# Two-layer decoder trunk: the high and low parts of an activation in one 512-column product

## The chip, the cores and the metric

The kernel runs on one core of one Trainium2 chip. Its time is the device time of one execution in microseconds (us); three executions of the kernel before took 362.71, 362.89 and 363.04 us, and 362.89 is the median that the changed kernel is held against. The profile is of one further execution; times in it count from its first instruction.

TensorE is called PE below (its loading of a stationary operand is PEld), VectorE DVE, ScalarE ACT, GpSimd POOL and the engine that issues the loads SP.

## The reference

256 tokens, model width 1024, two layers, all in float32. Each layer normalises the residual stream x, projects it, mixes tokens causally, multiplies by a SiLU gate z, projects back and adds; then a per-layer embedding p, projected to the model width, is gated by a sigmoid of the normalised stream and added:

```python
for i in range(DEPTH):
    h = rms_norm(x, norm_gain[i])
    x = x + (moba_layer(h, ...) if i % 2 == 0 else nsa_layer(h, ...))   # ends in: o @ w_out
    gate = jax.nn.sigmoid(rms_norm(x, ple_gate_gain[i]) @ ple_w_gate[i])
    x = x + gate * (p[i] @ ple_w_proj[i])
```

Layer 0 mixes with MoBA, which at 256 tokens is one causal block of 256 per head (16 heads of 64). Layer 1 mixes with NSA: a compressed branch, a selected-block branch and a window branch, gated per head; four groups of four heads share keys and values. Layer 1's softmax work is twice that of layer 0: two score matrices per head.

## The kernel before, in words

**Products in three parts.** A float32 weight W and a float32 activation X are each split into a high part, rounded to the fp32r type that PE multiplies in one pass, and a low part, the rest. The product is the sum of high W by high X, high W by low X and low W by high X. Weights are loaded 512 KB at a time into one of five `raw` tiles; ACT writes `hi` (five tiles), DVE subtracts and writes `lo` (five tiles); this is the "weight split". Activations are split likewise into `ah` and `al`, 128 features by 256 tokens each, nine tiles of either.

**Two kinds of products.** Those with tokens on the rows of the output (the projections to q, k and v) keep X still and stream 512 columns of W. Those with features on the rows (z, the projection of p, the output projection `o` and the gate `g`) keep a 128x128 block of W still and stream the 256 tokens of X, three products per block: lines 529 to 545, in class `Unit`. Such a unit makes 512 features out of eight k-blocks, in two PSUM banks `mm` of the four, each bank holding two 128-feature rows of results of 256 columns. The second gate unit of a layer (`apart=True`) holds its four rows in two `mm` banks and two score banks `s`.

**Evacuations.** `add_out` adds a bank of 512 columns of an `o` unit to x with one DVE instruction. `gate` multiplies a bank by the norm's factors `bc` (DVE), takes tanh (ACT), combines with the projected p and adds to x (DVE twice).

**What sets the order.** The program is written as a string of steps, `PROGRAM`, of which each records instructions. `w:o0.1` loads and splits the second weight block of layer 0's first output unit, `o0.1` multiplies with it, `o0>0` adds its first bank to x, `o0/1` is the rest of a unit for one bank; names of layer 1 begin with n. A planner (class `Plan`) then sets the order of each engine: it takes the step order as priority, gives each instruction a cost and a latency from its tables, and at each moment starts what can start first; copies marked as movable go to ACT or DVE as the planner chooses. Engines run their queues in order, so an early place in the DVE queue delays all that stands behind it. The steps are, for layer 0: the projections, `S` (scores and softmax), `T` (scaling and transposes), `V` (product with v), z, `x.k` (multiply by the gate and split), `o`, `b` (the norm), `y.k` (split for the gate), `g`; then `next.k` splits the stream for layer 1. Layer 1 runs `0S0` to `3S3`, `0T0` to `3T3`, the compression steps `KC`, `KD`, `W`, `WE`, and its own z, o and g.

In the transposes of layer 1, `sm` holds softmax weights, which DVE or ACT scale by `l1` (class `Group`, method `trans`) before PE transposes them. All the instructions carry line 396, a helper that emits them, so tiles' names tell them apart.

Of the kernel before, what the change touches and what calls it, by code (L numbers as in the profile page):

```python
# [8 lines left out]
F32R = mybir.dt.float32r  # L9
AF = mybir.ActivationFunctionType  # L10
OP = mybir.AluOpType
AX = mybir.AxisListType

P = 128
T = 256
D = 1024
KT = 8
# [2 lines left out]
SWITCH, POW = 150.0, 2300.0  # L20
NRAW, NHI, NLO, NPT, NA = 5, 5, 5, 9, 9
WARM = 16
MARGIN = 100.0

PROGRAM = ("x0 w:c0 x2 c0 x1 w:c1 c1 x3 w:c2 c2 x4 w:c3 w:c4 x5 c3 w:c5 w:k.0 x6 w:c6 consts x7 k.0 w:c7 c4 w:k.1 c5 "
# [22 lines left out]

STORES = 5

# [8 lines left out]
class View:  # L59


    def __init__(self, tile_, ap, steps=()):
        self.tile, self.ap, self.steps = tile_, ap, steps
# [354 lines left out]
def trunk(ctx: ExitStack, tc: tile.TileContext, a, out):  # L418
# [77 lines left out]
        return (hi.rearrange("p (a b) -> p a b", a=shape[0]), lo.rearrange("p (a b) -> p a b", a=shape[0]))  # L496

    def split_act(src, gain=None, either=False):
        hi = apool.tile([P, T], F32R, tag="ah", name="ah")
        lo = apool.tile([P, T], F32R, tag="al", name="al")  # L500
        if gain is None:
            nc.scalar.activation(hi, src, AF.Copy)
            nc.vector.tensor_tensor(lo, src, hi.bitcast(F32), op=OP.subtract)
        else:
            if either:
                nc.copy(hi, src, gain)
            else:
                nc.scalar.activation(hi, src, AF.Copy, scale=gain)
            nc.vector.scalar_tensor_tensor(lo, src, gain, hi.bitcast(F32), op0=OP.mult, op1=OP.subtract)
        return hi, lo  # L510

    class Unit:

# [15 lines left out]
            self.w[g] = split(self.src[g], (self.kg, self.n))  # L529

        def mul(self, w, j, k, b, ms=(0, 1), cols=None, parts=(0, 1, 2)):
            (wh, wl), (xh, xl) = w, self.xs[k]
            first, last = k == 0, k == self.nk - 1
            if self.feat:
                for m in ms:
# [6 lines left out]
            else:  # L542
                c0, c1 = cols or (0, self.n)
# [17 lines left out]
        def steps(self, name):  # L561

            for g in range(self.granules):
                todo[f"w:{name}.{g}"] = lambda g=g: self.weights(g)
                if g < self.whole:
                    todo[f"{name}.{g}"] = lambda g=g: self.step(g)
            for i in range(len(self.parts)):
                todo[f"{name}/{i}"] = lambda i=i: self.part(i)
            return self

    todo = {}
# [115 lines left out]
    def evac_z(zz, u, i, m, norm):  # L687
# [4 lines left out]
        nc.scalar.activation(th, zr, AF.Tanh, scale=0.5)  # L692
        nc.vector.scalar_tensor_tensor(flat(zz[:, m:m + 2]), flat(th), 1.0, flat(zr), op0=OP.add, op1=OP.mult)

    def tail(i, oT, pvs, zin, xz, norm, after):


# [27 lines left out]
        def add_out(u, b, m):  # L725
            nc.vector.tensor_tensor(flat(xT[:, m:m + 2]), flat(xT[:, m:m + 2]), u.ps[b], op=OP.add)

        def split_g(k):
            xg[k] = split_act(xT[:, k], pg[:, i, k:k + 1])

# [19 lines left out]
                    after(k)  # L750

        for h in range(2):
            u = Unit(zin[h], True, xz).steps(f"{n}z{h}")
            for b in range(2):
                todo[f"{n}z{h}>{b}"] = lambda u=u, b=b, m=4 * h + 2 * b: evac_z(zz, u, b, m, norm)
            u = Unit(a["ple_proj"][i, h], True, px, nk=2).steps(f"{n}p{h}")
            for b in range(2):
                todo[f"{n}p{h}>{b}"] = lambda u=u, b=b, m=4 * h + 2 * b: evac_p(u, b, m)
            u = Unit(a["w_out"][i, h], True, xo, close=2).steps(f"{n}o{h}")
            for b in range(2):  # L760
                todo[f"{n}o{h}>{b}"] = lambda u=u, b=b, m=4 * h + 2 * b: add_out(u, b, m)
            u = Unit(a["ple_gate"][i, h], True, xg, apart=h == 1, close=i if h else 2).steps(f"{n}g{h}")
            for j in range(len(u.parts)):
                todo[f"{n}g{h}>{j}"] = lambda u=u, j=j, m=4 * h + (j if h else 2 * j), w=2 - h: gate(u, j, m, w)
# [576 lines left out]
def _arrays(i):  # L1341
    import numpy as np

    def c(v):
        return np.ascontiguousarray(v)
# [31 lines left out]
    r["w1"] = c(i["nsa_cmp_w1"][0].reshape(2, 4, 4, P, 256).transpose(0, 1, 3, 2, 4).reshape(2, 4, P, 1024))  # L1377
    r["w2"] = c(i["nsa_cmp_w2"][0].reshape(2, 2, P, HD).transpose(2, 1, 0, 3))

    r["cst"] = _constants()  # L1380
    return r

# [58 lines left out]
```

## Time and profile before

| | |
|---|---|
| median of three runs | 362.89 us (362.71 to 363.04) |
| profiled execution, first to last instruction | 359.3 us; no other time of that execution is given |
| what the runs' median has beyond that span | 3.6 us |
| PE busy | 353.5 us, 98% |
| DVE busy | 323.9 us, 90% |
| ACT busy | 270.6 us, 75% |
| read from and written to HBM | 57.5 and 1.0 MB, 163 GB/s over the span |

A row of a group gives line, engine, operation, tiles written and read, shape, count, then the busy time, the mean duration in ns and the idle time of the engine before it with what ended that. Matmuls overlap in the records: a 256-column product is recorded with 283 ns or so, and the next starts long before its end, so that the distance from start to start is what one costs. A row of a timeline gives the start, the duration, the engine and the instruction, and behind it in brackets the idle time before. A row of stretches gives the busy time of each engine within a stretch of the span.

### The profile page before, as it was taken

What the parts mean: (1) busy time and instruction counts of PE and PEld (TensorE: products, weight loads), DVE (VectorE), ACT (ScalarE), POOL (GpSimd) and SP (SyncE); (2) the same over time, 40 slices, a digit from 0 to 9 for tenths busy, and PEclk for the clock granted to TensorE, in tenths of its full rate; (3) what the DMA queues carried; (4) which work ended last, traced back from release to release, by engine and by line L of the source; (5) the groups of instructions that cost most, each with busy time, mean ns of one, the idle gap of its engine ahead of it and who ended that gap; (6) DMA issues with size and microseconds to landing.
All of it is one profiled execution on the core that took longest, in us unless ns stands there. A gap on an engine that the chain in (4) does not pass through costs nothing.

```text
span 359.3 us, 7138 instructions
## 1 busy us (share of the span) xinstructions
PE 353.5 (98%) x2569; PEld 321.3 (89%) x2569; DVE 323.9 (90%) x799; ACT 270.6 (75%) x592; POOL 29.2 (8%) x26
## 2 busy tenths in 40 slices
PE   8999999999999999999999999999999999999995
PEld 6788888888999999999889998777998999999995
DVE  5999999999999975969999999989999999967965
ACT  5756699986999855937665699959978989956711
POOL 1034004300000000000003300003000000000010
PEclk9999999999999999999999999999999999999999
DMA  7987656433564353645643645177374333142112
GB/s 241 386 313 244 188 186 224 166 117 108 191 193 130 116 177 98 218 153 177 205 141 113 210 120 174 60 291 280 133 232 150 119 126 111 52 146 98 59 31 88
DMA packets 20771, 58.97 MB, mean 164 GB/s; under 512 B 2560, under 2 KB 6016, under 8 KB 20736
## 3 DMA queue, kind: packets, MB, share of 16 engines
q1 hardware_dynamic: 20160, 58.04, 48.9%
q10 hardware_dynamic: 576, 0.48, 0.4%
q8 instruction: 20, 0.33, 0.4%
q14 instruction: 15, 0.12, 0.1%
HBM read 57.46 MB, written 1.05 MB: 163 GB/s over the span
## 4 chain that ended last, share of the span: by engine, by line
PE 96%; DMA 2%; DVE 0%; SPq 0%; issue 0%; ACT 0%; DVEq 0%; ACTq 0%
PE mm L396 74%; PE tr L396 13%; PE s L396 10%; DMA tmp<-in_moba_in 1%; DMA gain_in<-in_gain_in 1%; DVE tmp L396 0%; SPq L396 0%; DVE hi L396 0%; ACT tmp L396 0%; DVEq L1436 0%; DVE xT L396 0%; ACTq L396 0%
## 5 line engine op out<-in xcount | busy, mean ns | idle before, releaser
L396 ACT ACTIVATE hi<-raw 128x1024 fp32r<-128x1024 f32 (+2 forms) x100 | 99.0, 1006 | 29.8 <-PE mm L396 22.3
L396 DVE TENSOR_TENSOR lo<-raw,hi 128x1024 fp32r<-128x1024 f32 (+2 forms) x100 | 115.1, 1159 | 5.5 <-ACT hi L396 4.5
L396 PE MATMUL mm<-al,hi 128*128 128x256 f32 x416 | 116.9, 287 | 0.0
L396 PE MATMUL mm<-ah,lo 128*128 128x256 f32 x416 | 114.5, 286 | 0.0
L396 PE MATMUL mm<-ah,hi 128*128 128x256 f32 x416 | 114.3, 286 | 0.0
L396 PEld LDWEIGHTS mm<-al,hi 128*128 128x128 f32 x416 | 79.3, 191 | 0.2
L396 PEld LDWEIGHTS mm<-ah,lo 128*128 128x128 f32 x416 | 78.0, 191 | 0.3
L396 PEld LDWEIGHTS mm<-ah,hi 128*128 128x128 f32 x416 | 77.8, 191 | 0.4 <-issue 0.2
L396 PE MATMUL mm<-hi,ah 128*128 128x512 f32 (+2 forms) x178 | 66.7, 379 | 0.5 <-ACT ah L396 0.4
L396 PE MATMUL mm<-hi,al 128*128 128x512 f32 (+2 forms) x178 | 66.1, 374 | 0.0
L396 PE MATMUL mm<-lo,ah 128*128 128x512 f32 (+2 forms) x178 | 63.8, 375 | 0.0
L396 ACT ACTIVATE sm<-sm,nb 128x128 f32<-128x128 f32 (+1 forms) x96 | 42.6, 446 | 6.6 <-DVE nb L396 6.2
L396 PEld LDWEIGHTS mm<-hi,ah 128*128 128x128 f32 x178 | 33.4, 188 | 6.4 <-DVE hi L396 0.7
L396 PEld LDWEIGHTS mm<-hi,al 128*128 128x128 f32 x178 | 33.4, 188 | 5.4 <-DVE al L396 0.2
L396 PEld LDWEIGHTS mm<-lo,ah 128*128 128x128 f32 x178 | 33.1, 188 | 5.4 <-DVE lo L396 0.3
L396 DVE CUSTOM_DVE_ANT_0 sm<-s,cst,nr_q 128x128 f32<-128x128 f32 (+1 forms) x96 | 36.2, 410 | 1.6 <-PE s L396 1.3
L396 ACT ACTIVATE pt<-tr 128x384 f32<-128x384 f32 x48 | 21.6, 482 | 3.9 <-PE tr L396 3.6
L396 PE MATMUL tr<-cst,sm 128*128 128x128 f32 x144 | 23.9, 274 | 0.0
L396 POOL TENSOR_TENSOR r_q<-r,neg_half 128x16 f32<-128x16 f32 x5 | 15.8, 3150 | 76.9 <-DVE r L396 76.9
L396 ACT ACTIVATE tmp<-tmp 128x512 f32<-128x512 f32 (+3 forms) x22 | 11.2, 517 | 13.6 <-DVE tmp L396 13.5
L396 PEld LDWEIGHTS tr<-cst,sm 128*128 128x128 f32 x144 | 17.1, 140 | 2.0 <-issue 0.4
L396 ACT ACTIVATE ah<-xT,gain_in 128x256 fp32r<-128x256 f32 x31 | 14.8, 499 | 4.8 <-DVE xT L396 3.7
(176 smaller groups left out, 535.0 us busy)
## 6 DMA issues: line engine op xcount, KB each, us to landing
raw<-in_moba_in SPq DMA_DIRECT2D x28, 512.0 KB, 4.4
raw<-in_nsa_in SPq DMA_DIRECT2D x24, 512.0 KB, 3.7
raw<-in_w_out SPq DMA_DIRECT2D x16, 512.0 KB, 3.5
raw<-in_ple_gate SPq DMA_DIRECT2D x16, 512.0 KB, 3.9
raw<-in_w SPq DMA_DIRECT2D x8, 512.0 KB, 4.1
raw<-in_ple_proj SPq DMA_DIRECT2D x4, 512.0 KB, 4.1
raw<-in_nsa_vs SPq DMA_DIRECT2D x4, 304.0 KB, 2.8
xT<-in_x SPq DMA_DIRECT2D x8, 128.0 KB, 3.8
```

Of the source, the lines that this page charges most:

```text
L396: getattr(getattr(self.nc, o.engine), o.method)(*[real(x) for x in o.args], **{k: real(x) for k, x in o.kwargs.items()})
```

## The change

The output projections `o0`, `o1`, `no0`, `no1` and the gates `g0`, `g1`, `ng0`, `ng1` are made by a new class `Wide`. High and low part of an activation now lie side by side in one tile `a` of 512 columns, and the high block of W is multiplied with both at once: one 512-column product into one whole PSUM bank (high-by-high in the first half, high-by-low in the second) and one 256-column product of the low block into the first half. A unit makes 256 features in two banks and takes two weight blocks; there are 16 of them, named `o0a`, `o0b` and so on. The last, `ng1b`, is left narrow: it streams high and low part one after the other into the same half. The two halves of a bank have to be added: `add_wide` adds each half to x with an instruction of its own; `gate_wide` copies the second half to SBUF (ACT), adds the first (DVE), and goes on as before, 256 columns at a time instead of 512 or 256. Weights of these units come from arrays laid out for them, 512 KB a load as before. z and the projection of p stay as they were.

The step order is new from the 61st step on; below stand two of its lines.

```diff
+WIDE, NARROW = "o0 o1 g0 g1 no0 no1 ng0 ng1", "ng1b"
...
-           "no1.1 no1/0 no1>0 ny.4 w:ng0.1 nb.1 w:ng1.1 w:ng1.2 nb.3 no1/1 no1>1 ny.7 nb.5 ng0.0 ny.3 ng0.1 nb.6 "
+           "nb.6 nb.7 ng0a.00 nb w:ng0b.0 ny.7 ny.5 w:ng0a.1 ng0b.00 w:ng1a.0 ng0a.01 ny.4 ng0b.01 ny.6 w:ng0b.1 ng0b.10 "
...
     def split_act(src, gain=None, either=False):
-        hi = apool.tile([P, T], F32R, tag="ah", name="ah")
-        lo = apool.tile([P, T], F32R, tag="al", name="al")
+        both = apool.tile([P, 2, T], F32R, tag="a", name="a")
+        hi, lo = both[:, 0], both[:, 1]
...
-        return hi, lo
+        return hi, lo, both.rearrange("p a b -> p (a b)")
...
+    class Wide:
+        def __init__(self, src, xs, wide=True):
+            self.src, self.xs, self.w, self.ps, self.wide = src, xs, {}, None, wide
+
+        def weights(self, g):
+            if self.ps is None:
+                self.ps = [bank("mm", 4) for _ in range(2)]
+            self.w[g] = split(self.src[g], (4, T))
+
+        def mul(self, g, m):
+            (wh, wl), s, o = self.w[g], slice(m * P, m * P + P), self.ps[m]
+            for j in range(4):
+                k = 4 * g + j
+                xh, xl, both = self.xs[k]
+                if self.wide:
+                    nc.tensor.matmul(o, wh[:, j, s], both, start=k == 0, stop=False, skip_group_check=True)
+                else:
+                    nc.tensor.matmul(o[:, :T], wh[:, j, s], xh, start=k == 0, stop=False, skip_group_check=True)
+                    nc.tensor.matmul(o[:, :T], wh[:, j, s], xl, start=False, stop=False, skip_group_check=True)
+                nc.tensor.matmul(o[:, :T], wl[:, j, s], xh, start=False, stop=k == KT - 1, skip_group_check=True)
...
+        def add_wide(u, b, m):
+            for c in (slice(0, T), slice(T, 2 * T)):
+                nc.vector.tensor_tensor(xT[:, m], xT[:, m], u.ps[b][:, c], op=OP.add)
+
+        def gate_wide(u, b, m):
+            ps, x, last = u.ps[b], xT[:, m], i == 1 and m == KT - 1
+            gr, th = tmp("gr")[:, :T], tmp("th")[:, :T]
+            for c, d in (((slice(0, P), slice(T, T + P)), (slice(P, T), slice(T + P, 2 * T))) if last
+                         else ((slice(0, T), slice(T, 2 * T)),)):
+                if u.wide:
+                    nc.scalar.activation(gr[:, c], ps[:, d], AF.Copy)
+                    nc.vector.tensor_tensor(gr[:, c], gr[:, c], ps[:, c], op=OP.add)
+                nc.vector.tensor_tensor(gr[:, c], gr[:, c] if u.wide else ps[:, c], n1.bc[:, c], op=OP.mult)
+                nc.scalar.activation(th[:, c], gr[:, c], AF.Tanh, scale=0.5)
+                nc.vector.scalar_tensor_tensor(th[:, c], th[:, c], 1.0, pp[:, m, c], op0=OP.add, op1=OP.mult)
+                nc.vector.tensor_tensor(x[:, c], x[:, c], th[:, c], op=OP.add)
+                if last:
+                    (nc.scalar if c.start else nc.sync).dma_start(out[:, m, c], xT[:, m, c])
...
```

Three places show what this makes of the engines' queues. Before, PE's queue in the first output unit of layer 0 holds triples: high and low part of an activation (`ah`, `al`) with a high weight block (`hi`), and the high part with the low block (`lo`), into one bank `mm`.

```order
L396 MATMUL mm_79<-ah_106,hi_127 128x256
L396 MATMUL mm_79<-al_115,hi_127 128x256
L396 MATMUL mm_79<-ah_106,lo_132 128x256
L396 MATMUL mm_81<-ah_106,hi_127 128x256
L396 MATMUL mm_81<-al_115,hi_127 128x256
L396 MATMUL mm_81<-ah_106,lo_132 128x256
```

Now, in the first output unit of layer 0, it holds pairs, with transposes of softmax weights (`tr<-cst,sm`) between the groups as before.

```order
L399 MATMUL tr_76<-cst_65,sm_70 128x128 x3
L399 MATMUL mm_80<-a_106,hi_118 128x512
L399 MATMUL mm_80<-a_106,lo_123 128x256
L399 MATMUL mm_80<-a_108,hi_118 128x512
L399 MATMUL mm_80<-a_108,lo_123 128x256
L399 MATMUL mm_80<-a_107,hi_118 128x512
L399 MATMUL mm_80<-a_107,lo_123 128x256
```

Two products of 256 columns became one of 512 in each pair; over the program 480 became 240, and nothing else of PE's queue changed in number.

The second place is the end of layer 1's attention on DVE: the last softmax work of the last group (`ISA sm`: a score block shifted and reduced), the last scalings by `l`, and weight splits (`lo<-raw,hi`). Before:

```order
L396 TENSOR_TENSOR lo_132<-raw_134,hi_127 128x1024
L396 ISA sm_68,nb_3_184<-s_165,cst_65,nr_q_156 128x128
L396 ISA nb_3_184 128x1
L396 ISA sm_68,nb_3_184<-s_166,cst_65,nr_q_156 128x256
L396 ISA nb_3_184 128x1
L396 TENSOR_TENSOR al_114<-big_90,ah_105 128x256
L396 TENSOR_TENSOR lo_130<-raw_137,hi_125 128x1024
L396 RECIPROCAL l_3_188<-l_3_188 128x4
L396 TENSOR_TENSOR al_115<-big_90,ah_113 128x256
L396 TENSOR_TENSOR l_3_188<-l_3_188,gt_104 128x4
L396 TENSOR_SCALAR sm_70<-sm_70,l_3_188 128x128
```

Now:

```order
L399 TENSOR_SCALAR sm_69<-sm_69,l_2_178 128x256
L399 TENSOR_TENSOR l_3_179<-l_3_179,gt_104 128x4
L399 TENSOR_SCALAR sm_72<-sm_72,l_3_179 128x128
L399 TENSOR_SCALAR sm_72<-sm_72,l_3_179 128x256
L399 TENSOR_SCALAR sm_71<-sm_71,l_3_179 128x128
L399 TENSOR_SCALAR sm_71<-sm_71,l_3_179 128x256
L399 TENSOR_TENSOR tmp_86<-mm_78,bc_135 128x512
L399 TENSOR_TENSOR lo_121<-raw_124,hi_117 128x1024
```

The weight splits between the last scores moved behind them. Counted over the DVE queue, of the 105 weight splits 75 stand before the first softmax instruction of layer 1 in both orders; 21 stood between that and the last scaling, now 17; 9 stood behind, now 13.

The third place is the gates of layer 1 on DVE behind the norm's factors, `bc`. Before, a gate is a product with `bc`, a combination with the projected p (`big`) and an addition to x, and no weight split stands behind `bc`:

```order
L396 COPY bc_144<-tr_75 128x256
L396 TENSOR_TENSOR tmp_86<-mm_78,bc_144 128x256
L396 TENSOR_TENSOR tmp_82<-mm_81,bc_144 128x256
L396 SCALAR_TENSOR_TENSOR tmp_85<-tmp_85,big_88 128x256
L396 SCALAR_TENSOR_TENSOR tmp_84<-tmp_84,big_88 128x256
L396 TENSOR_TENSOR xT_63<-xT_63,tmp_85 128x256
L396 TENSOR_TENSOR xT_63<-xT_63,tmp_84 128x256
L396 TENSOR_TENSOR tmp_83<-mm_79,bc_144 128x512
```

Now:

```order
L399 COPY bc_135<-tr_75 128x256
L399 TENSOR_TENSOR tmp_86<-tmp_86,mm_81 128x256
L399 TENSOR_TENSOR tmp_86<-tmp_86,bc_135 128x256
L399 SCALAR_TENSOR_TENSOR tmp_84<-tmp_84,big_88 128x256
L399 TENSOR_TENSOR tmp_82<-tmp_82,mm_80 128x256
L399 TENSOR_TENSOR xT_63<-xT_63,tmp_84 128x256
L399 TENSOR_TENSOR tmp_82<-tmp_82,bc_135 128x256
L399 TENSOR_TENSOR lo_119<-raw_126,hi_114 128x1024
```

Each gate has one more DVE instruction, and one weight split, for the last unit `ng1b`, stands between them. Behind `bc` DVE's queue holds 27 instructions of 256 columns, 6 of 128 and this split; it held 9 of 256 columns, 6 of 512 and 6 of 128.

More of the change, by code (lines that the diff above doesn't have):

```diff
@@ L22 @@
 WARM = 16
+WIDE, NARROW = "o0 o1 g0 g1 no0 no1 ng0 ng1", "ng1b"
 MARGIN = 100.0
-PROGRAM = ("x0 w:c0 x2 c0 x1 w:c1 c1 x3 w:c2 c2 x4 w:c3 w:c4 x5 c3 w:c5 w:k.0 x6 w:c6 consts x7 k.0 w:c7 c4 w:k.1 c5 "
[22 rows of a table removed]
+PROGRAM = ("x0 w:c0 x2 c0 x1 w:c1 c1 x3 w:c2 c2 x4 w:c3 w:c4 x5 c3 w:c5 w:k.0 x6 w:c6 consts x7 k.0 w:c7 c4 w:k.1 c5 a.1 a.3 "
[24 rows of a table added]
 STORES = 5
@@ L531, in mul @@
         def mul(self, w, j, k, b, ms=(0, 1), cols=None, parts=(0, 1, 2)):
-            (wh, wl), (xh, xl) = w, self.xs[k]
+            (wh, wl), (xh, xl, _) = w, self.xs[k]
             first, last = k == 0, k == self.nk - 1
@@ L568, in steps @@
                 todo[f"{name}/{i}"] = lambda i=i: self.part(i)
+            return self
+    class Wide:
[16 more added lines that the diff above has]
+                nc.tensor.matmul(o[:, :T], wl[:, j, s], xh, start=False, stop=k == KT - 1, skip_group_check=True)
+        def steps(self, name):
+            for g in range(2):
+                todo[f"w:{name}.{g}"] = lambda g=g: self.weights(g)
+                for m in range(2):
+                    todo[f"{name}.{g}{m}"] = lambda g=g, m=m: self.mul(g, m)
             return self
@@ L693, in evac_z, with evac_wz @@
         nc.vector.scalar_tensor_tensor(flat(zz[:, m:m + 2]), flat(th), 1.0, flat(zr), op0=OP.add, op1=OP.mult)
+    def evac_wz(zz, ps, m, norm):
+        zr, th = tmp("zr")[:, :T], tmp("th")[:, :T]
+        nc.scalar.activation(zr, ps[:, T:], AF.Copy)
+        nc.vector.tensor_tensor(zr, zr, ps[:, :T], op=OP.add)
+        nc.vector.tensor_tensor(zr, zr, norm.bc, op=OP.mult)
+        nc.scalar.activation(th, zr, AF.Tanh, scale=0.5)
+        nc.vector.scalar_tensor_tensor(zz[:, m], th, 1.0, zr, op0=OP.add, op1=OP.mult)
     def tail(i, oT, pvs, zin, xz, norm, after):
@@ L726, in add_out, with wide @@
             nc.vector.tensor_tensor(flat(xT[:, m:m + 2]), flat(xT[:, m:m + 2]), u.ps[b], op=OP.add)
+        def add_wide(u, b, m):
[15 more added lines that the diff above has]
+                    (nc.scalar if c.start else nc.sync).dma_start(out[:, m, c], xT[:, m, c])
+            if not last:
+                after(m)
+        def wide(kind, h, xs, evac):
+            name = f"{n}{kind}{h}"
+            if name not in WIDE.split():
+                return False
+            for q in range(2):
+                u = Wide(a["w_" + name][q], xs, name + "ab"[q] not in NARROW.split()).steps(name + "ab"[q])
+                for b in range(2):
+                    todo[f"{name}{'ab'[q]}>{b}"] = lambda u=u, b=b, m=4 * h + 2 * q + b: evac(u, b, m)
+            return True
         def split_g(k):
@@ L752, in tail @@
         for h in range(2):
-            u = Unit(zin[h], True, xz).steps(f"{n}z{h}")
-            for b in range(2):
-                todo[f"{n}z{h}>{b}"] = lambda u=u, b=b, m=4 * h + 2 * b: evac_z(zz, u, b, m, norm)
+            if not wide("z", h, xz, lambda u, b, m: evac_wz(zz, u.ps[b], m, norm)):
+                u = Unit(zin[h], True, xz).steps(f"{n}z{h}")
+                for b in range(2):
+                    todo[f"{n}z{h}>{b}"] = lambda u=u, b=b, m=4 * h + 2 * b: evac_z(zz, u, b, m, norm)
             u = Unit(a["ple_proj"][i, h], True, px, nk=2).steps(f"{n}p{h}")
@@ L758, in tail @@
                 todo[f"{n}p{h}>{b}"] = lambda u=u, b=b, m=4 * h + 2 * b: evac_p(u, b, m)
-            u = Unit(a["w_out"][i, h], True, xo, close=2).steps(f"{n}o{h}")
-            for b in range(2):
-                todo[f"{n}o{h}>{b}"] = lambda u=u, b=b, m=4 * h + 2 * b: add_out(u, b, m)
+            if not wide("o", h, xo, add_wide):
+                u = Unit(a["w_out"][i, h], True, xo, close=2).steps(f"{n}o{h}")
+                for b in range(2):
+                    todo[f"{n}o{h}>{b}"] = lambda u=u, b=b, m=4 * h + 2 * b: add_out(u, b, m)
+            if wide("g", h, xg, gate_wide):
+                continue
             u = Unit(a["ple_gate"][i, h], True, xg, apart=h == 1, close=i if h else 2).steps(f"{n}g{h}")
@@ L1378, in _arrays @@
     r["w2"] = c(i["nsa_cmp_w2"][0].reshape(2, 2, P, HD).transpose(2, 1, 0, 3))
+    w = {}
+    for l, (n, z, lo) in enumerate((("", i["moba_w_in"][0], 3072), ("n", i["nsa_w_in"][0], 2608))):
+        w[n + "z"], w[n + "o"] = z[:, lo:lo + D], (i["moba_w_out"], i["nsa_w_out"])[l][0]
+        w[n + "g"] = i["ple_w_gate"][l]
+    for name in WIDE.split():
+        v = w[name[:-1]][:, 512 * int(name[-1]):][:, :512]
+        r["w_" + name] = c(v.reshape(2, 4, P, 2, T).transpose(3, 0, 2, 1, 4).reshape(2, 2, P, 4 * T))
     r["cst"] = _constants()
```

44 rows, old and new, of the table PROGRAM are left out of this document.

## The prediction

> **What bounds the kernel now.** I read the page's busy shares and its chain of waits first.
>
> ```profile
> span 359.3 us, 7138 instructions
> PE 353.5 (98%) x2569; PEld 321.3 (89%) x2569; DVE 323.9 (90%) x799; ACT 270.6 (75%) x592; POOL 29.2 (8%) x26
> DVE  5999999999999975969999999989999999967965
> PE mm L396 74%; PE tr L396 13%; PE s L396 10%; DMA tmp<-in_moba_in 1%; DMA gain_in<-in_gain_in 1%; DVE tmp L396 0%; SPq L396 0%; DVE hi L396 0%; ACT tmp L396 0%; DVEq L1436 0%; DVE xT L396 0%; ACTq L396 0%
> ```
>
> The chain lies on PE for nearly all of the span, so a shorter PE queue shortens the kernel as long as PE is fed. But DVE is at 90%, and its digits show where it has room: slices 15 to 18 and 35 to 40, which are the output and gate stages of the two layers. Elsewhere it stands at nine tenths or more. So I cut the span where layer 1's attention starts and ends on DVE, at its first softmax instruction (214.4) and its last scaling (315.1), with the view of stretches (total, then busy time of PE, PEld, DVE, ACT, POOL; then the granted clock).
>
> ```profile
> 0.00:214.40 214.40, 212.86 (x1431) 192.62 (x1432) 196.06 (x412) 160.20 (x303) 23.58 (x20) 1.00 0.57 185
> 214.40:315.10 100.70, 100.61 (x799) 89.80 (x799) 97.45 (x331) 90.84 (x255) 4.00 (x5) 1.00 0.46 156
> 315.10:359.30 44.20, 39.99 (x343) 38.90 (x341) 30.44 (x59) 19.55 (x35) 1.61 (x1) 0.99 0.26 83
> ```
>
> The middle stretch is level between two engines: PE has no idle time and DVE only 3.25 of 100.7 us. What DVE waited for there is in the view of waits for that window:
>
> ```profile
> DVE sm L396 <- PE s L396: 1.3, 2, 1.0
> DVE l L396 <- ACT sm L396: 0.5, 1, 0.5
> DVE hl L396 <- ACT qk_0r L396: 0.3, 1, 0.3
> ```
>
> 1.3 us of the idle time is DVE waiting for PE; the other 1.95 are ACT and gaps of about 30 ns between its own instructions, and would be there with an infinitely fast PE. So DVE alone needs 97.45 + 1.95 = 99.4 us of the 100.7. In this stretch a shorter PE queue gains next to nothing. In the last one DVE has 30.44 of 44.2: there PE sets the end.
>
> **The change: PE.** A product's price is the distance from start to start.
>
> ```profile
> 353.97 0.28 PE L396 MATMUL s<-al,hi 128*128 128x256 f32 x1
> 354.09 0.28 PE L396 MATMUL s<-ah,lo 128*128 128x256 f32 x1
> 354.21 0.28 PE L396 MATMUL s<-ah,hi 128*128 128x256 f32 x1
> 227.57 0.39 PE L396 MATMUL mm<-hi,ah 128*128 128x512 f32 x1
> 227.80 0.39 PE L396 MATMUL mm<-hi,al 128*128 128x512 f32 x1
> 228.03 0.39 PE L396 MATMUL mm<-lo,ah 128*128 128x512 f32 x1
> 228.25 0.39 PE L396 MATMUL mm<-hi,ah 128*128 128x512 f32 x1
> ```
>
> 256 columns cost 0.120 us and 512 cost (228.25 - 227.57) / 3 = 0.227. Both carry a fixed 0.013: 256 columns are half of 512, and 2 x 0.120 - 0.227 = 0.013. Merging two into one saves that, 240 times: 16 units of 8 k-blocks and 2 rows are 256, less 16 in the narrow unit. **Gain: 240 x 0.013 = 3.1 us.** Weight loads (one less per pair) cost nothing in either: they run under the product before, since the distances above already hold one each.
>
> TensorE: Matmul & The Clock Gate in the Trainium skill, section "Wait — 56ns, not 53.3ns?", puts the fixed cost of a matmul at about 2.5 ns once the clock is full. By that the merging would save 0.6 us and not 3.1, an estimate from that page. The rows above disagree, at a granted clock of 1.00, and the rows decide.
>
> The new order also mixes PE's queue otherwise. Transposes of softmax weights stand between products in runs; counted from the order there are 89 runs of such float32 work before and 77 now. A run of 6 and one of 3:
>
> ```profile
> 226.00 0.39 PE L396 MATMUL mm<-lo,ah 128*128 128x512 f32 x1
> 226.23 0.82 PE L396 MATMUL tr<-cst,sm 128*128 128x128 f32 x6
> 226.80 0.48 PE L396 MATMUL mm<-hi,ah 128*128 128x512 f32 x1
> 318.01 0.29 PE L396 MATMUL mm<-ah,hi 128*128 128x256 f32 x1
> 318.13 0.49 PE L396 MATMUL tr<-cst,sm 128*128 128x128 f32 x3
> 318.38 0.36 PE L396 MATMUL mm<-al,hi 128*128 128x256 f32 x1
> ```
>
> Six in one run take 0.80 - 0.227 = 0.57; three take 0.37 - 0.12 = 0.25, so twice three 0.50. One run fewer costs 0.07, twelve 0.9. Where a run has to wait for its softmax weights the advantage of a further run is gone, so the bounds are 0 and 0.9, and I take **+0.6**, as most runs in the trace stand like these.
>
> **The change: DVE.** The groups of DVE and the one of ACT that stand for the new work:
>
> ```profile
> L396 DVE TENSOR_TENSOR lo<-raw,hi 128x1024 fp32r<-128x1024 f32 x88 | 106.5, 1219 | 5.3 <-ACT hi L396 4.5 <-PE mm L396 0.4
> L396 DVE TENSOR_TENSOR xT<-xT,mm 128x512 f32<-128x512 f32 x8 | 5.5, 684 | 5.1 <-PE mm L396 5.1
> L396 DVE TENSOR_TENSOR tmp<-mm,bc 128x256 f32<-128x256 f32 x4 | 1.6, 419 | 0.0
> L396 DVE SCALAR_TENSOR_TENSOR big<-tmp,tmp 128x512 f32<-128x512 f32 x8 | 5.5, 683 | 0.0
> L396 DVE TENSOR_SCALAR sm<-sm,l 128x128 f32<-128x128 f32 x34 | 9.1, 279 | 0.1
> L396 DVE TENSOR_TENSOR al<-big,ah 128x256 fp32r<-128x256 f32 x16 | 6.2, 415 | 0.3
> L396 ACT ACTIVATE tmp<-tmp 128x256 f32<-128x256 f32 x7 | 2.8, 408 | 6.0 <-DVE tmp L396 6.0
> ```
>
> Output units: 32 additions of 256 columns from PSUM in place of 8 of 512: 32 x 0.42 - 8 x 0.68 = +8.0 us. The nearest row for such an addition is the product with `bc`, which also reads one PSUM operand of 256 columns. Gates: 14 further additions, 5.9, and the three older instructions of each gate in pieces of 256 in place of some of 512, 3 x 0.6. In all **+15.7 us of DVE** (11.3 if each overlaps its neighbour's end by 0.1, as queued pairs do), 339 us of a span of some 358. ACT gets 14 copies, 14 x 0.4 = +5.6, at 75%. Half of the new work falls into each layer's output and gate stage.
>
> Does it fit? Layer 0: it lies in the first stretch, where DVE has 18.3 us idle; some 4.6 go to the start, and 8 are added. I cost it at nothing; the cover is about 5 us, and beyond that each us of DVE would be one of PE. Layer 1: the last stretch had 13.8 idle. There the new order puts 4 weight splits (9 to 13) and these 8 us, so DVE's 30.4 become about 42.5, and the stretch itself grows, since PE's work moves there too. PE counts by the order: the middle stretch loses 104 products of 256 columns and gains 9 of 512, 104 x 0.120 - 9 x 0.227 = 10.4 us, while in front of 214.4 nothing changes in sum (the merging there pays for work drawn forward). So the last stretch grows by 10.4 - (3.1 - 0.6) = 7.9 to some 52 us, and DVE with 42.5 still fits.
>
> The middle stretch is the dear one. DVE there loses 4 weight splits (4.9), 2 SiLU combinations (1.4), 1 product of z with its norm (0.7), 2 gated outputs and their 2 splits (1.7), and gains 3 scalings (0.8), 3 copies of the compressed branch, and one subtraction (1.5): 6.4 less by these rows, 5.8 where they overlap; I take 6.0. DVE then needs 99.4 - 6.0 = 93.4 us with all its gaps, 91.5 without. PE's own work there was at most 100.6 and is 10.4 less, 90.2; with its waits for runs taken out, my count by distances is 99.0 before and 88.6 now. Before, PE lost 100.7 - 99.0 = 1.7 us in this stretch; now between 91.5 - 88.6 = 2.9 and 93.4 - 88.6 = 4.8. So the added wait of PE is **+1.2 to +3.1**. I take +1.6, near the lower end: the last scalings now follow each other with no weight split between, so PE runs products under them.
>
> DMA moves nothing in sum: 142 issues on SP in both, with the same sizes, and the landings of 4 us lie behind five buffers. The wait that is added is PE's for DVE; queued behind it on PE are the products of z and o, which are those that fill the time, and behind DVE's scalings the weight splits that PE needs next.
>
> **Sum:** -3.1 + 0.6 + 1.6 = **-0.9 us**, 359.3 to 358.4 in the span. The runs' median lies 3.6 above the profiled span, so 362.0. By the bounds: -3.1 + 0 + 0 gives 359.8, and -3.1 + 0.9 + 3.1 gives 363.8.
>
> **The rivals.** *PE's whole saving arrives.* If the planner's tight queue hides DVE in the middle stretch (ACT's waits there belonged to single places and may go), the term of 1.6 is 0 to 0.3: -2.5, 360.4. For it: DVE's idle time of before holds no long wait. Against it: 88.6 of PE against 91.5 of DVE.
>
> *Nothing is left.* The stretch takes its upper bound, 93.4: -3.1 + 0.6 + 3.1 = +0.6, 363.5. For it: the small gaps were all there before.
>
> *Slower: DVE's gates at the end.* Behind the norm's factors DVE had little to do:
>
> ```profile
> 345.11 0.38 PE L396 MATMUL tr<-cst,rstd 128*128 128x128 f32 x2
> 345.52 0.42 DVE L396 COPY bc<-tr 128x256 f32<-128x256 f32 x1 [2.22 <-PE tr L396]
> 349.74 0.69 DVE L396 SCALAR_TENSOR_TENSOR tmp<-tmp,big 128x512 f32<-128x512 f32 x1 [0.76 <-ACT tmp L396]
> 352.46 0.69 DVE L396 SCALAR_TENSOR_TENSOR tmp<-tmp,big 128x512 f32<-128x512 f32 x1 [0.70 <-ACT tmp L396]
> 354.81 0.28 PE L396 MATMUL s<-ah,lo 128*128 128x256 f32 x1
> ```
>
> Now 27 instructions of 256 columns (10.0 to 11.3 us) and a weight split (1.2) come between `bc`, 0.8 behind the transposes, and the last half-rows of 128 columns: 12.0 to 13.3 us. PE has behind the same transposes 25 pairs, 2 single products and 48 narrow ones: 25 x 0.347 + 50 x 0.120 = 14.7. That leaves 1.4 to 2.7. If each of eight gates waits for its tanh or its copy on ACT as the two rows show, 0.5 on average, 4 us are needed and DVE ends 2 late: 362.0 + 2.2 = 364.2. It decides from some 0.3 us of wait per gate. Against it: the new queue interleaves two or three gates, so one's wait is another's work.
>
> *Merging saves little.* The rows for 0.120 and 0.227 show products among their own kind; here 512 and 256 columns alternate. If a product of 256 that follows one of 512 starts some 0.0105 later than these rows let it, 240 x 0.0105 = 2.5 us of the 3.1 are lost, and the sum is -0.6 + 0.6 + 1.6 = +1.6, 364.5. No row of before shows such a late start. The same time would follow from the 2.5 ns of the Trainium skill (TensorE: Matmul & The Clock Gate, section "Wait — 56ns, not 53.3ns?"); the trace so far speaks against it.
>
> **How the numbers follow.** Forecast 0.44 (its own range 361.2 to 362.8), whole saving 0.16, nothing left 0.16, gates at the end 0.17, merging saves little 0.03, something else and slower 0.04. A measurement here tells about 0.2%, 0.7 us, from no change, so faster is below 362.2 and slower above 363.6. Faster: 0.16 and two thirds of the forecast, 0.46. Slower: 0.17 + 0.03 + 0.04 and a fifth of "nothing left", 0.27. Same: 0.27. The range runs from the lower bound, 359.7, to 364.4, which takes in most of the slower case.
>
> **What would show it.** In the changed profile: PE with 240 products of 512 columns at 0.227 and 256 behind them at 0.120 (else the first term is wrong); between layer 1's first softmax and last scaling 93 us in place of 100.7 with DVE idle under 2 (else the third); DVE busy 335 to 340 in all; the tail from PE's last product to the end still near 4.5 (else the gates). If DVE waits for PE in the middle stretch, PE still sets it and the gain is larger; if PE's queue shows stalls in layer 0's gates, the cover of 5 us was not there.

## The result: 1.9 us faster, and the profile after

Beside the kernel before, the changed kernel took 359.74 us against 362.89: a ratio of 0.9933 (0.9907 to 0.9958). Two later comparisons gave 0.9950 (0.9932 to 0.9967; 359.95 against 361.60) and 0.9955 (0.9938 to 0.9973; 360.09 against 361.62). (Each ratio is an estimate over the executions of both kernels and need not equal the quotient of the two medians, which is 0.9913 in the first comparison.) Weighted by their intervals the three make 0.9949, 1.9 us with some 0.4 either way. Two executions of all that were made, one of the run `noscale` with 433 us at a granted clock of 0.75 and one of the kernel before with 1981 us, are left out of every ratio. The forecast was 0.9 us less, at 362.0, within 359.7 to 364.4.

The first profile of the changed kernel, from the page: span, busy times, DVE in 40 slices, the chain of waits by line.

```profile
span 359.6 us, 6744 instructions
PE 353.2 (98%) x2329; PEld 308.7 (86%) x2329; DVE 335.5 (93%) x849; ACT 275.3 (77%) x610; POOL 27.7 (8%) x26
DVE  5799999999999988989999999999999999989975
PE mm L399 71%; PE tr L399 12%; PE s L399 6%; DMA xT<-in_x 2%; DVE lo L399 2%; DMA gain_in<-in_gain_in 1%; DVE q L399 1%; SPq L399 0%; DVE tmp L399 0%; DVE k_1r L399 0%; DVE hl L399 0%; DVE ssq L399 0%; DVE k_0r L399 0%; DVE kd_0r L399 0%; DVE v_1r L399 0%
```

DVE has 11.6 us more (11.3 were counted with overlaps), its roomy slices of the output and gate stages are filled, and PE still stands at 98%. The span is no shorter than the 359.3 of before, though. The reason lies in the executions that were profiled. For each execution of the changed kernel span and time are both known, and the time is always 1.74 to 1.82 above the span: this one took 361.40, the longest of its five; the others took 359.12 to 360.61. The kernel before, profiled a second time, has a span of 359.9 at a time of 361.65, 1.75 apart as well. So 359.3 belongs to some 361.1 us: the execution shown ahead of the prediction was a quick one.

The view of stretches of the changed kernel shows where its first profile lost time (first 20 us, then to layer 1's first softmax, to its last scaling, to the end):

```profile
0.00:20.00 20.00, 17.95 (x78) 13.15 (x78) 14.26 (x34) 12.21 (x22) 0.99 (x9) 1.00 0.86 293
20.00:215.43 195.43, 195.43 (x1227) 173.25 (x1226) 186.69 (x400) 150.27 (x294) 21.72 (x11) 1.00 0.53 173
215.43:308.52 93.09, 92.90 (x728) 81.41 (x727) 91.71 (x327) 85.41 (x244) 4.07 (x5) 1.00 0.45 151
308.52:359.60 51.08, 46.90 (x303) 40.88 (x301) 42.80 (x91) 27.43 (x51) 0.88 (x1) 0.98 0.33 104
```

The same view of its second profile (an ordinary execution, 359.89 us):

```profile
0.00:20.00 20.00, 18.70 (x85) 14.75 (x86) 14.94 (x38) 12.28 (x23) 1.69 (x10) 1.00 0.89 317
20.00:213.94 193.94, 193.94 (x1219) 171.95 (x1218) 185.62 (x396) 149.93 (x294) 21.67 (x10) 1.00 0.53 171
213.94:307.02 93.08, 92.91 (x728) 81.47 (x727) 91.71 (x327) 85.35 (x244) 4.07 (x5) 1.00 0.45 151
307.02:358.10 51.08, 46.88 (x303) 40.87 (x301) 42.78 (x91) 27.36 (x51) 0.88 (x1) 1.00 0.32 104
```

And of the second profile of the kernel before:

```profile
0.00:20.00 20.00, 18.95 (x87) 15.57 (x88) 15.47 (x38) 12.81 (x24) 1.69 (x10) 1.00 0.91 324
20.00:214.29 194.29, 194.29 (x1345) 178.27 (x1345) 180.43 (x374) 147.38 (x280) 21.65 (x10) 1.00 0.52 171
214.29:315.71 101.42, 100.70 (x801) 89.76 (x800) 97.70 (x331) 90.92 (x254) 4.00 (x5) 1.00 0.44 154
315.71:359.90 44.19, 39.94 (x343) 38.85 (x341) 30.40 (x59) 19.55 (x35) 1.61 (x1) 0.98 0.27 84
```

The changed kernel's two profiles agree within 0.01 in the middle stretch (93.09, 93.08) and in the last one (51.08 twice). All of their difference, 1.49 of 1.5, lies ahead of it, where PE's busy time of the first 20 us differs by 0.75. So what happens ahead of layer 1's attention differs by up to 1.5 us from one execution to the next, and two single profiles can't be subtracted to better than that. Between the two ordinary ones the middle is 8.3 shorter, the last stretch 6.9 longer, the front 0.35 shorter: 1.8 together. PE is idle in the middle stretch for 0.17 us, DVE for 1.37.

### The profile page after: what moved, and what is told of

Its sections match the earlier page's. It is cut to its first block, busy times and chain, and to the rows that moved or that the text cites. A ratio compares the mean times of both kernels' runs of the same rounds, so it can differ in the third digit from the quotient of the medians.

```text
span 359.6 us, 6744 instructions
## 1 busy us (share of the span) xinstructions
PE 353.2 (98%) x2329; PEld 308.7 (86%) x2329; DVE 335.5 (93%) x849; ACT 275.3 (77%) x610; POOL 27.7 (8%) x26
## 4 chain that ended last, share of the span: by engine, by line
PE 89%; DVE 5%; DMA 3%; issue 1%; SPq 0%; ACT 0%; DVEq 0%; ACTq 0%
PE mm L399 71%; PE tr L399 12%; PE s L399 6%; DMA xT<-in_x 2%; DVE lo L399 2%; DMA gain_in<-in_gain_in 1%; DVE q L399 1%; SPq L399 0%; DVE tmp L399 0%; DVE k_1r L399 0%; DVE hl L399 0%; DVE ssq L399 0%; DVE k_0r L399 0%; DVE kd_0r L399 0%; DVE v_1r L399 0%
## 5 line engine op out<-in xcount | busy, mean ns | idle before, releaser
L399 PE MATMUL mm<-a,hi 128*128 128x256 f32 (+1 forms) x656 | 162.5, 328 | 0.0
L399 PE MATMUL mm<-a,lo 128*128 128x256 f32 x448 | 123.4, 284 | 0.0
L399 PEld LDWEIGHTS mm<-a,hi 128*128 128x128 f32 x656 | 108.9, 190 | 10.6 <-issue 0.2
L399 PE MATMUL mm<-hi,a 128*128 128x512 f32 (+2 forms) x356 | 104.5, 379 | 1.0 <-DVE hi L399 0.7
L399 PEld LDWEIGHTS mm<-a,lo 128*128 128x128 f32 x448 | 83.9, 190 | 0.8
L399 PEld LDWEIGHTS mm<-hi,a 128*128 128x128 f32 x356 | 63.8, 191 | 13.0 <-ACT hi L399 1.9
L399 PE MATMUL mm<-lo,a 128*128 128x512 f32 (+2 forms) x178 | 63.9, 374 | 0.0
L399 ACT ACTIVATE sm<-sm,nb 128x128 f32<-128x128 f32 (+1 forms) x96 | 42.6, 448 | 5.3 <-DVE nb L399 5.1
L399 PEld LDWEIGHTS mm<-lo,a 128*128 128x128 f32 x178 | 33.2, 188 | 5.3
L399 ACT ACTIVATE tmp<-tmp 128x256 f32<-128x256 f32 (+3 forms) x26 | 12.1, 470 | 12.7 <-DVE tmp L399 12.6
L399 DVE TENSOR_SCALAR sm<-sm,l 128x128 f32<-128x128 f32 (+1 forms) x72 | 18.9, 318 | 0.1
L399 ACT ACTIVATION_READ_ACCUMULATOR sm<-sm,nb 128x1 f32 x96 | 18.4, 192 | 0.0
```

The source lines that it names most:

```text
L399: getattr(getattr(self.nc, o.engine), o.method)(*[real(x) for x in o.args], **{k: real(x) for k, x in o.kwargs.items()})
```

## The experiments

The edits are shown shortened; `...` marks what is left out of them.

**The two kernels once more.**

> The kernel before, unchanged, to see a second profiled execution of it. In the five executions of the changed kernel the time lies 1.74 to 1.82 us above the span. The prediction put 3.6 between the span and the median of the kernel before. If that was right, a run of 362.9 has a span of 359.3. If the profiled execution of before was simply a quick one, the gap is 1.8 here too, a run of 362.9 has a span of 361.1, and the new profile shows where the quick one saved 1.8 us; the place expected is the first 20 us, where PE waits for the first loads and splits (2.9 us of PE's waits there before, 4.5 in the changed kernel).

Ratio 1.0003 (0.9987 to 1.0019), 361.50 us. The gap of 1.75 is the one of the changed kernel, not the 3.6 of the prediction. The place was missed: the first 20 us are like those of before. In the middle stretch the ordinary execution has one wait of PE that the quick one did not have:

```profile
PE tr L396 <- ACT big L396: 0.6, 1, 0.6
```

> The changed kernel, unchanged. Its profiled execution was the longest of five (span 359.6; the others 357.3 to 358.8). Expected: median near 359.7, and in the profile of an ordinary execution a first 20 us with less waiting of PE than 4.5 us. The rest of the profile (middle stretch, tail) should read within 0.3 us as in the first one.

> The changed kernel once more, beside the same runs of the kernel before as the three below: ratio 0.995 (0.993 to 0.997), and in its trace pairs of 0.353 us on the mean as in the two before.

Ratios 0.9950 and 0.9955, as expected. In all three profiles pairs that follow each other at once take 0.352 on the mean.

**The merging alone.** Every wide product is issued as two, and nothing else moves:

```diff
-  matmul(o, wh[:, j, s], both, start=k == 0)
+  matmul(o[:, :T], wh[:, j, s], xh, start=k == 0)
+  matmul(o[:, T:], wh[:, j, s], xl, start=k == 0)
```

> Only the merging is undone: each 512-column product becomes two of 256 columns with the same weights, into the two halves of the same bank; every other instruction and every queue is that of the changed kernel. The prediction's first term (0.013 us per merged pair, 240 of them, less nothing) expects +3.1 us, about 362.8. The distances in the changed kernel's trace (0.236 from a 512 to the 256 behind it, 0.118 on to the next 512, 0.354 per pair in place of 0.360) expect 240 x 0.006 = +1.4, about 361.1. With the 2.5 ns that the Trainium skill (TensorE: Matmul & The Clock Gate, section "Wait — 56ns, not 53.3ns?") gives as a matmul's fixed cost it would be +0.6.

This kernel is for timing alone, since each bank now has two starts; number, shapes and order of the instructions are the ones meant. Ratio 1.0002 (0.9990 to 1.0013), 361.58 us, 1.63 more than the changed kernel beside it. That is the effect of the merging: with it undone, new order and added evacuations together cost and bring nothing (0.0, within 0.4 us). The middle stretch, which holds few merged products, is as long as in the changed kernel (93.13 and 93.08); what the profile has more lies ahead of it (0.7) and behind it (0.8):

```profile
214.62:307.75 93.13, 92.95 (x737) 81.89 (x736) 91.73 (x327) 85.31 (x244) 4.07 (x5) 1.00 0.44 151
```

The rows agree. In this kernel (three rows to a k-block):

```profile
161.79 0.28 PE L402 MATMUL mm<-a,hi 128*128 128x256 f32 x1
161.91 0.28 PE L403 MATMUL mm<-a,hi 128*128 128x256 f32 x1
162.03 0.28 PE L405 MATMUL mm<-a,lo 128*128 128x256 f32 x1
162.15 0.28 PE L402 MATMUL mm<-a,hi 128*128 128x256 f32 x1
```

and in the changed kernel's second profile, first in its quickest place (143.72 to 144.76), then at the units shown above:

```profile
143.72 0.39 PE L399 MATMUL mm<-a,hi 128*128 128x512 f32 x1
...
144.07 0.39 PE L399 MATMUL mm<-a,hi 128*128 128x512 f32 x1
...
144.42 0.39 PE L399 MATMUL mm<-a,hi 128*128 128x512 f32 x1
...
144.76 0.39 PE L399 MATMUL mm<-a,hi 128*128 128x512 f32 x1
...
160.19 0.40 PE L399 MATMUL mm<-a,hi 128*128 128x512 f32 x1
160.42 0.28 PE L399 MATMUL mm<-a,lo 128*128 128x256 f32 x1
160.54 0.40 PE L399 MATMUL mm<-a,hi 128*128 128x512 f32 x1
160.78 0.28 PE L399 MATMUL mm<-a,lo 128*128 128x256 f32 x1
160.90 0.40 PE L399 MATMUL mm<-a,hi 128*128 128x512 f32 x1
161.13 0.28 PE L399 MATMUL mm<-a,lo 128*128 128x256 f32 x1
161.25 0.40 PE L399 MATMUL mm<-a,hi 128*128 128x512 f32 x1
```

A triple takes 0.360. Three pairs take 161.25 - 160.19 = 1.06, 0.353 each, and they repeat as 0.350, 0.361, 0.349; at 144 they take (144.76 - 143.72) / 3 = 0.347, the prediction's price, with the same forms and tiles. Of the 211 pairs that another one follows at once, 38 go at 0.348 or less, 168 at 0.349 to 0.365, and 5, behind transposes, at 0.43 or more. The first two sorts take 0.352 on the mean: 240 x (0.360 - 0.352) = 1.9 us, beside the 1.6 by the times.

**Can the lost half of the merging be had?** First the four wide products of a half-unit ahead of its four narrow ones:

```diff
-  for j in range(4): matmul(o, wh[:, j, s], both); matmul(o[:, :T], wl[:, j, s], xh)
+  for j in range(4): matmul(o, wh[:, j, s], both)
+  for j in range(4): matmul(o[:, :T], wl[:, j, s], xh)
```

> The four 512-column products of a half-unit go first, then its four 256-column products, in place of one after the other in turn; nothing else moves. If a 256 behind a 512 starts 0.009 late and the 512 behind a 256 0.002 early because the shapes alternate, three of four such changes go: 180 pairs x 0.007 = -1.3 us, 358.4. If the prediction's price of 0.347 a pair holds however they stand, 359.7, no change.

Ratio 0.9969 (0.9956 to 0.9981), 360.36 us: no gain. It is 0.4 us more than the changed kernel beside it, but the intervals of the two ratios overlap. The rows start 1.40 apart per half-unit of four pairs, 0.350 a pair:

```profile
160.30 1.09 PE L408 MATMUL mm<-a,hi 128*128 128x512 f32 x4
...
161.70 1.09 PE L408 MATMUL mm<-a,hi 128*128 128x512 f32 x4
...
163.10 0.40 PE L408 MATMUL mm<-a,hi 128*128 128x512 f32 x1
```

Against the slow cycle 180 pairs x 0.003 = 0.5 us would be gained. But a half-unit now needs four activation tiles at its start instead of one: the wide product behind the one at 314.98 us waits for its tile, which DVE writes, and starts 0.46 later instead of 0.23:

```profile
315.44 0.30 PEld L408 LDWEIGHTS mm<-a,hi 128*128 128x128 f32 x2 [0.50 <-DVE a L408]
```

Whether more than that eats the gain isn't settled. Second, the low block's product ahead of the high block's:

```diff
-  matmul(o, wh[:, j, s], both); matmul(o[:, :T], wl[:, j, s], xh)
+  matmul(o[:, :T], wl[:, j, s], xh); matmul(o, wh[:, j, s], both)      # k > 0
```

> In each pair but the first of a unit's row the 256-column product of the low block goes ahead of the 512-column product of the high block; every other queue is the same. In the traces of the changed kernel a pair takes 0.353 us in most places (0.350, 0.361, 0.349 in turn) and 0.3465 in a few. If the extra 0.0067 belongs to the order within a pair, pairs fall to 0.347 and the time by 210 x 0.0067 = 1.4 us (ratio 0.991). If it belongs to streams of 512 columns with a changing stationary block of weights, whatever stands ahead, the pairs stay at 0.353 and the ratio at 0.995.

This kernel, too, is for timing alone, since the mark that ends a sum now has one more product behind it. Ratio 1.0002 (0.9990 to 1.0014), 361.75 us. Undisturbed pairs took 0.351 on the mean, so neither theory's figure; and the time rose. The first row of PE's waits shows why:

```profile
PE mm L406 <- DVE lo L406: 1.7, 2, 0.9
```

The high part is there 1.2 us before the low one, which DVE makes from it. With the high block first, its product covers that split; turned round, PE waited twice, 0.8 and 0.9 us, in each layer once. That is the size of the 1.7 us to the changed kernel.

**What DVE costs.** Three kernels with the order frozen and one thing taken from or given to DVE. The additions first (in the gates the one left out is that of the first half, the larger part of the sum, which is the same for the time):

```diff
-  vector.tensor_tensor(xT[:, m], xT[:, m], ps[:, T:], op=add)
-  vector.tensor_tensor(gr, gr, ps[:, :T], op=add)
```

> The changed kernel with its order frozen, but the 30 additions of the second halves are left out (16 in the output units, 14 in the gates), so that the product of the high block with the low activation is missing from x; 30 x 0.42 = 12.6 us less for DVE, all in the output and gate stages. PE's work is the same. The prediction costed these additions at nothing, because DVE has room there: then the ratio to the kernel before stays at 0.995 (359.9 where before is 361.6). If the new order gains something that the additions eat up, it falls by 1 us or more, below 0.992.

Ratio 0.9954 (0.9938 to 0.9970), 360.35 against 361.96 us: no gain, and no change beyond the interval of 0.6 us either way. DVE is busy for 325.9 us in all, 9.2 less than in the changed kernel's second profile (its instructions overlap by some 0.1, so that 30 of them are worth less than 12.6). In the last stretch DVE has 38.55 busy in place of 42.78, and the stretch is as long as before:

```profile
307.54:358.70 51.16, 46.89 (x303) 40.87 (x301) 38.55 (x76) 27.04 (x51) 0.88 (x1) 0.99 0.33 103
```

Then half of DVE's scalings in layer 1:

```diff
-  vector.tensor_scalar(sm[:, c], sm[:, c], l1, op0=mult)        # every second one
```

> The changed kernel with its order frozen, but every second of the scalings of softmax weights that stand on DVE in layer 1 is left out (20 of them, some 6 us of DVE in the middle stretch), so that these weights are not divided by their sums. PE's work is the same. The prediction had DVE set the middle stretch with 1.6 us of added waits on PE: then some 1.6 us are gained, about 358.3 where the changed kernel takes 359.9 (ratio 0.991). If PE fills the stretch whatever DVE needs (its waits there are 0.2 us in the second profile), at most 0.3 is gained (0.994 to 0.995).

Ratio 0.9947 (0.9930 to 0.9964), a median of 360.22 us: nothing gained by some 6 us less of DVE in the middle, within 0.6. (Every second scaling of the changed kernel's second profile sums to 6.2 us.)

And more work for DVE there:

```diff
   vector.tensor_tensor_reduce(sm, s, ...)                       # behind every sixth
+  vector.tensor_tensor(spare[:, :T], spare[:, T:], spare[:, T:], op=add)
```

> The changed kernel with its order frozen and 11 additions of 256 columns put on DVE in the middle stretch, into a tile that nobody reads there, one behind every sixth softmax instruction: 11 x 0.42 = 4.6 us. In the second profile DVE has 1.4 us idle in this stretch of 93.1. If DVE sets it, 4.6 less at most 1.4 reach the end: +3.2 to +4.6, 363.1 to 364.5 where the changed kernel takes 359.9. If PE has a reserve there, as its 0.2 us of waits say, half or less comes through: up to +2.3.

Ratio 1.0030 (1.0017 to 1.0043), 362.78 us, 2.9 above the changed kernel's 0.995. Its middle stretch:

```profile
214.19:310.32 96.13, 95.43 (x728) 81.64 (x727) 95.08 (x338) 86.12 (x244) 4.07 (x5) 1.00 0.44 146
```

The 11 additions take 0.42 each, 4.6, but since they overlap with their neighbours DVE is busy for only 95.08 - 91.71 = 3.4 us more. Of these 3.05 come through and 0.3 go into its idle time. That is just under the first theory's 3.2 and above the second's 2.3. So both engines are full in this stretch: less DVE gains nothing, and more of DVE comes through nearly whole.

The row says something of reading profiles, too. PE has the same 728 products in the stretch as in the changed kernel, yet it is recorded as busy for 2.5 us longer, and its idle time rises only from 0.17 to 0.70. A 256-column product is recorded with 0.28 us where the next can start after 0.12, so a wait of up to 0.16 us leaves no gap in the records. So a PE without idle time can still have waited; what settles it here are the two runs, not the record.

**Narrow units in the new order.**

```diff
-NARROW = "ng1b"
+NARROW = "o0a o0b o1a o1b g0a ... ng1a ng1b"
```

> The new order of steps with all 16 units narrow: three products of 256 columns into one half of a bank, no copy and no second addition; the plan is made anew for it. Beside the run in which only the merging was undone (ratio 1.000) this takes away 16 + 14 additions on DVE and 14 copies on ACT. If these are free, as the prediction costed them, the ratio is 1.000 too (361.6). If they cost what the new order gains, it is below 0.997 (360.5 or less).

Ratio 1.0222 (1.0197 to 1.0246), 370.63 us. The kernel was not what the expectation says: its output units still added the second half of each bank, into which nothing had been multiplied, so that only the gates' 14 additions and copies went. And the plan came out another way. The middle stretch has PE idle for 4 us, and the first row of PE's waits there is for a DVE instruction that writes `tmp`:

```profile
213.97:312.50 98.53, 94.54 (x709) 81.89 (x708) 95.03 (x330) 84.54 (x242) 4.06 (x5) 0.97 0.45 148
```
```profile
PE mm L399 <- DVE tmp L399: 1.9, 1, 1.9
```

It says nothing on the price of the evacuations (the run without additions does), but it shows that an order of steps that suits one set of instructions can be 8 to 9 us worse with another. Whether the old order could carry merged products wasn't tried: a wide unit needs two banks for half as many features, so the old interleaving of two units may not fit into four banks and five weight tiles.

**Going further.**

```diff
-WIDE = "o0 o1 g0 g1 no0 no1 ng0 ng1"
+WIDE = "z0 z1 o0 o1 g0 g1 no0 no1 ng0 ng1"        # and z0a, z0b, z1a, z1b in the steps
```

> The two z projections of layer 0 are merged as well (four units of 256 features, 128 pairs), planned anew; each of eight rows gets a copy on ACT and an addition on DVE more (about 8 x 0.58 = 4.6 us of DVE in layer 0's attention). By the price measured on the outputs and gates, 128 x 0.0067 = -0.9 us: ratio 0.9925 if DVE has that room in layer 0. If DVE sets that place as it nearly does in layer 1, where 4.6 us more cost 2.9, the ratio is 1.000 or above.

Ratio 1.0157 (1.0129 to 1.0185), 367.40 us, 7.3 above the changed kernel beside it. PE's longest waits are now in layer 0's attention and at the start:

```profile
PE mm L401 <- DVE tmp L401: 2.3, 3, 1.3
PE tr L401 <- ACT sm L401: 2.1, 1, 2.1
PE mm L401 <- ACT a L401: 1.6, 1, 1.6
```

From 90 to 130 us PE is busy for 35.1 of 40 at a granted clock of 0.96, where the changed kernel's third profile has 40.0 at 1.00 (the first row is of the kernel with merged z):

```profile
90.00:130.00 40.00, 35.09 (x223) 30.71 (x222) 37.40 (x107) 35.73 (x89) 0.00 (x0) 0.96 0.41 136
90.00:130.00 40.00, 40.00 (x330) 38.18 (x329) 38.03 (x98) 37.53 (x87) 0.00 (x0) 1.00 0.49 166
```

The z units stand beside the softmax work, where DVE is busy for 38 of 40 us in the changed kernel. That it has no room there for an addition per row is the likely cause, but not a shown one: the order was planned anew as well, and no run separates the two.

```diff
-NARROW = "ng1b"
+NARROW = ""
```

> The last unit is merged too: 16 more pairs, 16 x 0.0067 = -0.1 us on PE, but the last gate gets a copy on ACT and an addition on DVE for each of its pieces, behind PE's last product. From the gate's rows a copy of 128 to 256 columns takes 0.3 to 0.4 us and an addition as much, so +0.5 to +0.7 at the end: ratio 0.996 to 0.997 where the changed kernel has 0.995. If these are hidden behind the store, no change.

Ratio 0.9974 (0.9958 to 0.9989), 360.69 us, 0.6 above the changed kernel beside it, as expected, though the two intervals overlap. The rows show the difference. From PE's last product to the store there are now

```profile
354.29 0.28 PE L399 MATMUL mm<-a,lo 128*128 128x256 f32 x1
354.60 0.45 ACT L399 ACTIVATE tmp<-mm 128x128 f32<-128x128 f32 x2 [0.47 <-PE mm L399]
...
355.07 0.48 DVE L399 TENSOR_TENSOR tmp<-tmp,mm 128x128 f32<-128x128 f32 x2
...
357.12 0.35 ACTq L399 DMA_DIRECT2D out<-xT  x1
```

2.83 us, where the changed kernel has 357.12 - 355.14 = 1.98:

```profile
355.14 0.28 PE L399 MATMUL mm<-a,lo 128*128 128x256 f32 x1
355.46 0.49 DVE L399 TENSOR_TENSOR tmp<-mm,bc 128x128 f32<-128x128 f32 x2 [0.81 <-PE mm L399]
...
357.12 0.35 ACTq L399 DMA_DIRECT2D out<-xT  x1
```

The tail is 0.85 longer for the 0.1 that merging saves: the last unit is better narrow. No kernel tried here is faster than the changed one.

## Why the prediction was right in its range and short of the gain

**The range.** 359.74 is in the stated range by 0.04 us. The working's own lower bound, -3.1 + 0 + 0, is 359.8, and the range was then written from 359.7; the first measurement lies between the two. That it fell inside is luck. By the 1.9 us of all three comparisons the time would be 361.0, well inside.

**The base, 3.6 us between span and median.** Only 1.8 of it is the distance from span to time; the other 1.8 is that the profiled execution was quicker than the median. The forecast change doesn't hang on this, since 359.3 + 3.6 is 362.9 again however the 3.6 is made up. What suffered is the reading of the profile: single waits and stretches of a quick execution were taken for the ordinary ones (100.7 in the middle, where the second profile has 101.4). Of the 2.3 us by which 362.0 missed 359.74, 1.0 is the error of the forecast change (0.9 for 1.9). The rest belongs to the first comparison, whose medians stand 3.1 us apart, where those of the later two stand 1.7 and 1.5 apart; why isn't known.

**Gain 240 x 0.013 = 3.1.** The sign and the place were right, the size was not: 1.6, by the run that undoes it alone, and 0.352 for 0.360 in the rows. The term that was mis-sized is the price of a 512-column product. The prediction took 0.227 from rows in which such a product stands among its own kind, and said that no row of before shows a 256-column product starting late behind a 512-column one. There are such rows:

```profile
217.58 0.28 PE L396 MATMUL mm<-al,hi 128*128 128x256 f32 x1
217.70 0.40 PE L396 MATMUL mm<-hi,ah 128*128 128x512 f32 x1
217.94 0.52 PE L396 MATMUL mm<-ah,lo 128*128 128x256 f32 x3
```

Here the next product starts 0.234 behind, and in the 19 undisturbed places of that profile where a 512-column product stands behind a 256-column and ahead of a 512-column one, 0.232 on the mean. By 0.232 the gain would have been 240 x (2 x 0.120 - 0.232) = 1.9. So the rival "merging saves little" was half true, for the reason it gave: in the changed kernel the 256-column product starts 0.23 to 0.24 behind the wide one. The Trainium skill's 2.5 ns for a matmul's fixed cost (TensorE: Matmul & The Clock Gate, section "Wait — 56ns, not 53.3ns?") would make it 0.6, an estimate from that page; the measured 1.6 is 6.7 ns a pair, between that 2.5 and the 13 that products among their own kind show.

**Runs of transposes, +0.6.** No run tests it alone. The traces bear out its size: taking for each run of float32 transposes the distance from the product ahead to the product behind, less the price of the product ahead, the 90 runs of before sum to 41.8 us in the quick profile, and the 78 runs, with as many transposes, to 42.6 in all three of the changed kernel. That is 0.9, the upper bound. In the ordinary profile of before, however, they sum to 42.5, for the one wait of 0.6 us for ACT's `big` stands in such a run. Against that the new order costs 0.1. How often the old order has this wait two profiles can't tell; it may be where the 0.6 is given back.

**DVE in the middle stretch, +1.6.** The stretch came out as forecast: 93.1 us for "93 in place of 100.7", DVE idle for 1.4, "under 2", DVE in all at 335. But taking DVE work away gained nothing, so the added wait of PE for DVE was not there. The step that failed is PE's own work there, 88.6: a count between two places in PE's queue. In time PE gets farther ahead by the end of the stretch. Placing the queue's products by the records, 372 of 256 columns and 48 of 512 lie within it before, 289 and 52 now: 83 x 0.120 - 4 x 0.227 = 9.1 less instead of 10.4, and 7 transposes more (0.8), 8.3 less in sum. The stretch lost 7.6 against the quick profile and 8.3 against the ordinary one, so that 0 to 0.7 of added wait is left. What was booked as waiting is products drawn forward. This is the rival "PE's whole saving arrives": its condition came true (DVE hides), and its 0.16 was too little; its figure of 2.5 us was not reached because the saving itself was half.

**Evacuations at nothing.** Right for the additions: leaving out all 30 that were new changed the ratio by 0.2 us, with an interval of 0.6 either way. The 14 copies on ACT were not tested alone. **Gates at the end.** Did not happen. DVE's waits for ACT there in the changed kernel's second profile are

```profile
DVE tmp L399 <- ACT tmp L399: 2.5, 6, 0.5
```

2.5 us over eight gates, about the 0.3 per gate from which this rival would have begun to tell; from the end of PE's last product to the end of the span it is 4.2 us in both kernels. The rival "nothing left" fell with the middle stretch.

So two errors of opposite sign nearly met: the merging was taken 1.5 too large, order and DVE 2.2 too dear (forecast +2.2, measured 0.0 within 0.4). That the sum came within 1 us of the measured change is luck in part. The chances for faster (0.46) were too low by the second error.

## What to carry to other kernels

Hold a sum against the time of the profiled execution itself, and profile the base twice: the distance between span and time is steady (1.74 to 1.82 us here), but single executions differ by as much as a small change is worth. Price a merged instruction from rows in its own mix of shapes, even where a profile has only a few of them: here 0.232 in place of 0.227 takes the gain from 3.1 us to 1.9. Where two engines are both full over a stretch, a count of one engine's queue between two landmarks is not a wait: test by taking work from one and by adding some, since the stretch can answer to the one and not to the other. And a product recorded for longer than the next has to wait hides short waits: a busy share near 100% is no proof that PE is fed.

## What the runs showed of the hardware that was not expected

The pair of a 512- and a 256-column product runs in two steady ways with the same forms and tiles: some 0.347 us, and a cycle of 0.350, 0.361, 0.349. The slower way holds in 168 to 173 of 206 undisturbed pairs in each of the three profiles of the changed kernel, and in 170 both with 30 additions less on DVE and with 11 more. The quick pairs stand at the same places of PE's queue each time (143.72 in the second profile, 145.2 in the first), so chance doesn't choose them. The kernel before has the like among its 512-column products: behind 256-column ones, from 169.91 us of its profile on, five start 0.233, 0.236, 0.229, 0.232 and 0.231 apart, and from then on 0.227. Neither with the four wide products first nor with the low block first do the pairs come down to 0.347 on the mean (0.350 to 0.352). What starts the one or the other is open.
